# One inference step of a hybrid decoder layer: gate tiles in other buffers, a distance before one small sum, a fifth buffer for raw weights

## Chip, core and metric

The kernel runs on one core of one Trainium2 chip. The metric is the device time of one execution in microseconds (us). The engines are named as the profile names them: PE is TensorE, PEld its weight loads, DVE is VectorE, ACT is ScalarE, POOL is GpSimd and SP is SyncE, which here only issues DMAs.

## What is computed

One layer of a decoder for 512 prompt positions and 8 sampled positions that share all weights. Cut to what matters:

```python
xn = rmsnorm(h, norm_mix);  z = xn @ w_in
q, k, v of attention = parts of z (with rope);  o_a = dilated windowed attention, three groups mixed by softmax of lse
qm, km = silu(causal_conv(z parts));  vm, og = sigmoid(part of z);  i and f gates = 8 columns of z
C, n, m = stabilised mLSTM update;  hm = num / max(|den|, exp(-m));  o_b = rmsnorm(hm) * mh_norm * og
h += (sigmoid(z_ga) * (o_a @ w_proj_a) + sigmoid(z_gb) * (o_b @ w_proj_b)) @ w_out
x = rmsnorm(h, norm_ffn);  h += (silu(x @ w_gate) * (x @ w_up)) @ w_down
h += sigmoid(rmsnorm(h, norm_ple) @ w_ple_gate) * (p @ w_ple_proj);  y = rmsnorm(h, norm_final)
```

Beside y it returns the new key and value caches, the convolution rows and the mLSTM states of the prompt and of each sampled row.

## The kernel before

All activations lie transposed: 128 features on the partitions, 520 columns (512 prompt, 8 samples) along the free axis. Each float32 product is made of three PE products in the fp32r type: weight and activation are each split into a high part (a rounded copy, `whi`, `xnh`) and a low part (source minus high part, `wlo`, `xnl`), and high by high, high by low and low by high are summed in PSUM. So every chunk of weights (128x512) costs one cast on ACT or DVE and one subtraction on DVE before PE can use it, and every activation likewise.

The instruction order is not written by hand. A program, called the planner here, walks through a list of dense jobs (`order`, filled by `job`, `group` and `wino`) in `dense_to`. Beside that, generators (`Procs`) hold all the rest: evacuations, norms, attention, the mLSTM. Each generator yields a condition, and the planner goes on with it when the condition holds; it looks at them twice in every k step of a dense job (a k step is three products in two column halves, six matmuls). The conditions are made by `on(engines, *tiles, **rooms)`: there must be room in the named buffers, and all tiles must be ready by the time of the first named engine in the planner's own clock (`Clock`). For "pe" that time is the planner's PE time now. On the chip each engine then runs its own queue strictly in that order, and semaphores make it wait where the planner was too early. `used[tag]` counts the tiles of a buffer that are in use; `free(n, tag)` gives them back; a tag that is not in `used` is not counted.

The stages in order: the gate columns and four output gates on the unnormalised input (`n_pre`), with the squares of the eight input tiles for the first norm beside it (`first_norm`); `w_in` for attention and for the four mLSTM heads; eight `w_in` tiles of the mixing gates, whose Tanh goes to buffers by `RING` (`ev_tanh`); `w_proj_a` (`j_pa`, two chunks of two k steps in all) and `w_proj_b` in the form of seven products for two by two blocks (`wino`, `PRODS`), four groups q = 0 to 3, with eight more gate tiles after q = 0 and q = 1; `w_out`; `w_gate` and `w_up`; `w_down`; the last gate and the last norm.

Names that the steps touch:
- 24 small matmuls on `onesr` at the start keep PE busy until data is there.
- `first_norm`: for each input tile `xr[k]` one Square on ACT and one addition on DVE, then the norm `r0`, on which the first evacuations (`th<-pp,rb`) wait; two PSUM pairs (`pp`) are all that there is.
- `ev_tanh(tag, key)`: Tanh from PSUM into a tile of buffer `tag`, then the PSUM pair is free. For P1 and P2 it first waits until the sample states of head 3 have been loaded (`("loads", 3)`), since P1 and P2 hold the rows qb and kb for them.
- `on` and `op`: hold the attention outputs `o_sb` and `oaf`; later two tiles of `mix` each, and `hid` in the feed-forward part.
- `mk_oa` splits `oaf` into `oah` and `oal`.
- `sample_sums(h)`: for each head, the tile `nt` (five small DVE operations after the last `numv`), summed over partitions by four PE matmuls on `ones`; then `dns` on ACT and DVE and `sample_out`, which finishes the sampled columns of the gated output `th`. `mk_ob` then scales `th` and makes the operand `piece`s of `w_proj_b`.
- Raw weights of `w_proj_b` come in four blocks per group (11, 12, 21, 22) into buffers that are taken in turn (`wraws`): two of `rp`, one `cA`, one `cB`. A block is loaded when its buffer's last user has been split (`wlast`) and when it is at most seven chunks ahead. From the blocks DVE makes sums (`ws<-raw`, `raw<-raw,ws`), since four of seven products take sums of blocks.

Of the kernel before, what the change touches and what calls it, by code (L numbers as in the profile page):

```python
# [228 lines left out]
def _body(nc, a, const, sb, psp, drp):  # L229
# [5 lines left out]
              P1=2, P2=2, cm=2, on=2, W0=2, W1=2, W2=2, W3=2, hm=2, sm=4, sm48=4,  # L235
              pp=2, b1=4, hf=3)
    WIDTH = dict(cA=640, cB=512, W1=384, W2=256, W3=128, raw=512, hi=512, lo=512, zc=ZC, yc=ZC - 3)
    used = dict.fromkeys(("pp", "G", "WK", "b1", "z", "y", "zc", "yc", "S", "P1", "P2", "cm", "hm", "hf", "sw", "rp"), 0)

    def tl(tag, name, shape=None, dt=F32, count=True):  # L240
        w = WIDTH.get(tag, 520)
        if tag in used and count:
            used[tag] += 1
        return ck.new(sb.tile(list(shape or (128, w)), dt, name=name, tag=tag, bufs=NB[tag]), tag, NB[tag])
# [18 lines left out]
    def free(n, tag):  # L263
        used[tag] -= n
# [2 lines left out]

    P = dict(PAR["A"])

    def on(engs, *tiles, lim=None, **rooms):  # L270

        engs = engs.split()

        def ok():
            for tag, n in rooms.items():
                if tag in used and used[tag] + n > NB[tag]:
                    return False
            now = ck.t["pe"]
            for tag, n in rooms.items():
                i = ck.count.get(tag, 0)  # L280
                if any(ck.idle(tag, i + j, NB[tag]) > now + P["SLACK"] for j in range(n)):
                    return False
            if engs[0] == "pe":
                t = now
            else:
                t = min(ck.t[e] for e in engs)
                if t > now + (P["LIM"] if lim is None else lim):
                    return False
                t = max(t, now) + 0.1
            return all(ck.ready(x) <= t for x in tiles)  # L290
        return ok
# [265 lines left out]
        yield lambda: not left[0]  # L557

    split_at, dma_at, prep_at = [0], [0], [0]
    wraws, wlast = [Cycle(["rp"] * 2 + ["cA", "cB"])], {}  # L560
    raws, parts, kept, wok = {}, {}, {}, {}

    def dma_chunk():
# [205 lines left out]
    flag = {}  # L769
# [19 lines left out]
    ml = {}  # L789
# [242 lines left out]
    def ev_tanh(tag, key, scaled=True):  # L1032
        room = {tag: 1} if tag in used else {}

        def gen(ps):
            if tag in ("P1", "P2"):
                yield lambda: ("loads", 3) in flag
            if scaled:
                yield on("act", ps, lim=P["EVLIM"], **room)
                t = tl(tag, "th", (128, 520))  # L1040
                S_.activation(p2(t), ps, AF.Tanh, scale=0.5)
                free(1, "pp")
            else:
                yield lambda: "r0" in flag
                yield on("dve", rb, lim=P["EVLIM"], **room)
                t = tl(tag, "th", (128, 520))
                V.tensor_tensor(p2(t), ps, p2(rb), op=ALU.mult)
                free(1, "pp")
                yield on("act", t)
                S_.activation(t, t, AF.Tanh, scale=0.5)  # L1050
            ml[key] = t
        return gen
# [396 lines left out]
    def sample_sums(h, numv):  # L1449

        nn = nout[:, h, :, 1:9]
        w_i = s24b[:, h, 8:16].unsqueeze(1).to_broadcast([128, 2, 8])
        w_x = s24b[:, h, 0:8].unsqueeze(1).to_broadcast([128, 2, 8])
        nt = small(32, "nt").rearrange("p (t c) -> p t c", t=2)
        tv = nt[:, :, 0:8]
        V.tensor_tensor(tv, qkm[:, h, 1], w_i, op=ALU.mult)
        V.tensor_tensor(nn, nst[:, h], w_x, op=ALU.mult)
        V.tensor_tensor(nn, nn, tv, op=ALU.add)
        V.tensor_tensor(tv, nn, qkm[:, h, 0], op=ALU.mult)
        V.tensor_tensor(nt[:, :, 8:16], numv, numv, op=ALU.mult)  # L1460
        yield on("pe", nt, b1=1)
        bk = bank((128, 16))
        for t in range(2):
            PE.matmul(bk, ones, nt[:, t], start=t == 0, stop=t == 1)

        dn = sb.tile([128, 16], F32, name="dns", tag="dns", bufs=2)
        yield on("act", bk)
        S_.activation(dn[:, 0:8], bk[:, 0:8], AF.Abs)
        V.tensor_copy(dn[:, 8:16], bk[:, 8:16])
        free(1, "b1")  # L1470
        yield on("dve", dn)
        V.tensor_tensor(dn[:, 0:8], dn[:, 0:8], s24b[:, h, 16:24], op=ALU.max)
        ml["ns", h] = True
        yield lambda: ("og", h, 0) in ml and ("og", h, 1) in ml
        yield from sample_out(h, numv, dn)

    def mlstm_prompt(h):
# [36 lines left out]
        for s in range(4):  # L1514
# [18 lines left out]
            hi = tl(f"W{s}", f"W{s}h", None, F32R)[:, :n]  # L1533
# [13 lines left out]
        for vt in range(2):  # L1547
            c = slice(128 * vt, 128 * vt + 128)
            yield on("pe", W[0][1], b1=2 - vt)
            nu = bank()  # L1550
            if vt == 0:
                dn = bank()
            for s, (hi, lo, n) in enumerate(W):
                yield on("pe", lo)
                vh, vl = (x[:, s % 2, c] for x in ml["vt", h][s // 2])
                for j, (l_, r_) in enumerate(((vh, hi), (vh, lo), (vl, hi))):
                    PE.matmul(nu[:, TP - n:TP], l_, r_, start=(s == 0 and j == 0), stop=(s == 3 and j == 2))
            if vt == 0:
                for s, (hi, lo, n) in enumerate(W):
                    yield on("pe")  # L1560
                    for j, r_ in enumerate((hi, lo)):
                        PE.matmul(dn[:, TP - n:TP], onesr, r_, start=(s == 0 and j == 0), stop=(s == 3 and j == 1))
            yield on("act dve", nu, hm=1, y=1)
            hm = tl("hm", "hm")
            sq = tl("y", "sqh", (128, 512))
            copy(hm[:, :TP], nu)
            S_.activation(sq, nu, AF.Square)
            free(1, "b1")
            nums.append(hm)
            if vt == 0:  # L1570
                sqh = sq
                yield on("act", dn)
                free(1, "cm")
                da = tl("cm", "da")
                S_.activation(da[:, :TP], dn, AF.Abs)
                free(1, "b1")
                yield on("dve", da, emb)
                V.tensor_tensor(da[:, :TP], da[:, :TP], emb, op=ALU.max)
            else:
                yield on("dve", sq)  # L1580
                add(sqh, sqh, sq)
                free(1, "y")
# [5 lines left out]
        hi, lo = (tl("y", "sqh" + x, (128, 512), F32R) for x in "hl")  # L1588
        split(hi, lo, sqh)
        free(1, "y")  # L1590
        yield on("pe", hi, lo, b1=1)
        bk = bank()
        PE.matmul(bk, onesr, hi, start=True, stop=False)
        PE.matmul(bk, onesr, lo, start=False, stop=True)
# [52 lines left out]
    X0, X = (lambda: xs0), (lambda: xs)  # L1647
# [37 lines left out]
    j_mo(2, 1)  # L1685
    j_mo(3, 0)
    j_mo(3, 1)
    RING = ("zc", "yc", "P1", "P2")
    for m in range(4):
        for w in range(2):  # L1690
            j_w(50 + 8 * w + m, ev_tanh(RING[m % 4], ("g", w, m)))
# [15 lines left out]
    V.memset(ones, 1.0)  # L1707

    wb = bank((128, 128))
    for _ in range(24):  # L1710
        PE.matmul(wb, onesr, onesr, start=True, stop=True)
    free(1, "b1")
    warm = const.tile([128, 1], F32, name="warm")
# [24 lines left out]
    def first_norm():  # L1738
        for k in range(KD):
            yield on("act", xr[k], y=1)  # L1740
            sq = tl("y", "sq")
            square(sq, xr[k])
            if k == 0:
                acc = sq
                continue
            yield on("dve", sq)
            add(acc, acc, sq)
            free(1, "y")
        yield from norm(acc, "r0")
        yield from renorm(xr, gmix, "X", xs)  # L1750
        free(8, "G")
        yield lambda: order_pos[0] >= n_pre
        for t in X0T:
            free(1, t)
# [27 lines left out]
    def mk_oa():  # L1782
        yield lambda: 1 in oaf and "oas" in flag and "state3" in flag
        for i in range(2):
            yield on("act dve", oaf[i], WK=2)
            hi = tl("WK", "oah", None, F32R)
            lo = tl("WK", "oal", None, F32R)
            split(hi[:, :TP], lo[:, :TP], oaf[i])
            split(hi[:, TP:], lo[:, TP:], oas[:, i])
            oa.append((hi, lo))  # L1790

    mhh = const.tile([128, 8], F32, name="mhh")
    V.tensor_scalar(mhh, mh, 0.5, None, op0=ALU.mult)
# [12 lines left out]
            yield on("act dve", og[1], **(dict(G=7) if h < 3 else dict(S=5, hm=2)))  # L1806
            yield from pieces(*og, tags, obp)

    mixtags = ["on"] * 2 + ["op"] * 2 + ["W0"] * 2 + ["cm"] * 2 + ["X"] * 8

    def ev_pa(m):
        def gen(ps):
# [29 lines left out]
    def mix_parts(t, m):  # L1842
        if m > 3:
            yield lambda: order_pos[0] >= n_gates[0]
        yield on("act dve", t)
        mixp[m] = [tl(tag, "mix", (128, 520), F32R) for tag in mixtags[2 * m:2 * m + 2]]
        split(*mixp[m], t)
        free(1, "y")
# [5 lines left out]
        return {f"{r + 1}{k + 1}": a[name][2 * q + r, k] for r in range(2) for k in range(2)}  # L1854

    wok["rp"] = lambda: ("loads", 3) in flag and used["rp"] == 0
    wok["cA"] = lambda: "scores" in flag and "oas" in flag and ("ns", 3) in ml and 1 in oaf
    wok["WK"] = lambda: order_pos[0] >= n_pa

# [463 lines left out]
```

## Time and profile before

| | |
|---|---|
| median of 3 runs | 1076.74 us (1074.07 to 1078.79) |
| profiled execution | 1074.97 us |
| its span, first to last instruction | 1073.2 us |
| PE busy | 1043.7 us (97%) |
| PEld, DVE, ACT busy | 1019.7, 850.1, 517.7 us |
| bytes moved by DMA | 180.21 MB, mean 168 GB/s |
| granted clock, mean | 0.994 |

How to read it: the busy time of PE counts matmuls from issue to modelled end. Where PE's row of waits names an engine and a tile, PE had nothing to run until that tile was there. The granted clock is 1.00 at 2.4 GHz and 0.50 at 1.2 GHz. All lines are those of one helper (L224), so instructions are told apart by their tiles.

### The profile page before, as it was taken

To read this page: it belongs to the slowest core of one execution; us is meant where nothing else is said; L and a number is where in the kernel's file an instruction comes from. 1 tells how busy PE (TensorE), PEld (TensorE's weight loads), DVE (VectorE), ACT (ScalarE), POOL (GpSimd) and SP (SyncE) were. 2 spreads that over 40 slices of the span, in tenths; PEclk is the share of its full clock that TensorE was granted. 3 is DMA by queue.
4 is the path that set the end of the run, shared out by engine and by line. 5 is a ranking of instruction groups with operands and counts; after the bars stand their busy time and mean duration, and the time that the engine had idled before them with its cause. 6 is when DMAs were issued, how large, how long until landed. Compare 5 with 4: busy or idle time off the path is not lost.

```text
span 1073.2 us, 21731 instructions
## 1 busy us (share of the span) xinstructions
PE 1043.7 (97%) x8408; PEld 1019.7 (95%) x8408; DVE 850.1 (79%) x1756; ACT 517.7 (48%) x974; POOL 28.0 (3%) x110
## 2 busy tenths in 40 slices
PE   9999999999999989998999999999999999999996
PEld 9999999899987989998999999999999999999995
DVE  6994578958797799897467588989788888866685
ACT  6534554555565566665333245444344334433552
POOL 0010010000110100000000000000000000000000
PEclk9999999999999989999999999999999999999999
DMA  7366258765865967974766733422332332333331
GB/s 246 109 184 203 89 165 270 241 214 184 266 216 178 289 242 255 330 240 167 257 201 231 257 114 94 148 80 70 119 112 71 118 110 73 112 90 106 99 110 60
DMA packets 91191, 180.21 MB, mean 168 GB/s; under 512 B 11636, under 2 KB 37796, under 8 KB 89680
## 3 DMA queue, kind: packets, MB, share of 16 engines
q1 hardware_dynamic: 90512, 178.29, 51.4%
q8 instruction: 66, 1.08, 0.4%
q10 hardware_dynamic: 576, 0.53, 0.1%
q14 instruction: 37, 0.30, 0.1%
HBM read 163.65 MB, written 59.13 MB: 208 GB/s over the span
## 4 chain that ended last, share of the span: by engine, by line
PE 79%; DVE 11%; DMA 6%; ACT 2%; issue 2%; SPq 1%; DVEq 0%; ACTq 0%
PE pp L224 46%; PE b L224 33%; DVE wlo L224 2%; DMA raw<-in_w_in 2%; DMA out_C_s<-ct 2%; DMA ct<-in_sC 1%; DVE yc L224 1%; DVE ct L224 1%; DVE Wf L224 1%; DVE junk L224 1%; SPq L224 1%; DMA out_kvout<-in_cache 1%; DVE sw L224 1%; ACT whi L224 0%; DMA kb<-mdr 0%
## 5 line engine op out<-in xcount | busy, mean ns | idle before, releaser
L224 DVE TENSOR_TENSOR wlo<-raw,whi 128x512 fp32r<-128x512 f32 (+3 forms) x359 | 236.5, 661 | 138.2 <-ACT whi L224 125.1
L224 ACT CAST whi<-raw 128x512 fp32r<-128x512 f32 (+3 forms) x336 | 199.9, 598 | 298.2 <-PE pp L224 155.7
L224 PE MATMUL b<-piece,whi 128*128 128x260 f32 x1176 | 214.7, 284 | 3.9 <-ACT piece L224 2.0
L224 PE MATMUL pp<-xnh,whi 128*128 128x260 f32 x992 | 205.0, 288 | 0.0
L224 PE MATMUL pp<-xnh,wlo 128*128 128x260 f32 x992 | 203.0, 286 | 0.0
L224 PE MATMUL pp<-xnl,whi 128*128 128x260 f32 x992 | 200.3, 283 | 0.0
L224 PEld LDWEIGHTS b<-piece,whi 128*128 128x128 f32 x1176 | 182.8, 190 | 4.7 <-ACT piece L224 2.3
L224 PE MATMUL b<-piece,wlo 128*128 128x260 f32 x588 | 167.3, 284 | 0.1
L224 PEld LDWEIGHTS pp<-xnh,whi 128*128 128x128 f32 x992 | 153.5, 190 | 2.3 <-issue 0.9
L224 PEld LDWEIGHTS pp<-xnh,wlo 128*128 128x128 f32 x992 | 153.6, 190 | 2.1 <-issue 0.9
L224 PEld LDWEIGHTS pp<-xnl,whi 128*128 128x128 f32 x992 | 154.0, 190 | 0.0
L224 PEld LDWEIGHTS b<-piece,wlo 128*128 128x128 f32 x588 | 111.5, 190 | 0.4 <-DVE wlo L224 0.4
L224 PE MATMUL pp<-hph,wlo 128*128 128x260 f32 x352 | 70.9, 283 | 0.0
L224 PE MATMUL pp<-hpl,whi 128*128 128x260 f32 x352 | 70.8, 283 | 0.0
L224 PE MATMUL pp<-hph,whi 128*128 128x260 f32 x352 | 70.8, 282 | 0.0
L224 PEld LDWEIGHTS pp<-hph,whi 128*128 128x128 f32 x352 | 54.3, 189 | 0.0
L224 PEld LDWEIGHTS pp<-hpl,whi 128*128 128x128 f32 x352 | 54.3, 189 | 0.0
L224 PEld LDWEIGHTS pp<-hph,wlo 128*128 128x128 f32 x352 | 54.3, 189 | 0.0
L224 ACT CAST whi<-ws 128x512 fp32r<-128x512 f32 x28 | 17.4, 622 | 57.6 <-PE b L224 48.7
L224 DVE SCALAR_TENSOR_TENSOR yc<-zc,par,yc 128x552 f32<-128x552 f32 x48 | 37.7, 785 | 6.0 <-ACT yc L224 5.4
L224 DVE TENSOR_TENSOR uv<-uv,b 128x260 f32<-128x260 f32 (+1 forms) x84 | 40.8, 486 | 0.0
L224 PE MATMUL b<-x3h,wlo 128*128 128x260 f32 x128 | 36.7, 287 | 0.0
(393 smaller groups left out, 1918.9 us busy)
## 6 DMA issues: line engine op xcount, KB each, us to landing
raw<-in_w_in SPq DMA_DIRECT2D x132, 256.0 KB, 3.5
out_kvout<-in_cache SPq DMA_DIRECT2D x64, 512.0 KB, 6.3
raw<-in_w_gate SPq DMA_DIRECT2D x44, 256.0 KB, 2.7
raw<-in_w_up SPq DMA_DIRECT2D x44, 256.0 KB, 4.1
ct<-in_sC SPq DMA_DIRECT2D x32, 256.0 KB, 5.3
out_C_s<-ct SPq DMA_DIRECT2D x32, 256.0 KB, 5.1
raw<-in_w_down SPq DMA_DIRECT2D x32, 256.0 KB, 2.7
out_kvout<-in_cache SPq DMA_DIRECT2D x16, 510.0 KB
```

What stands on the lines that cost most here:

```text
L224: fn(*args, **kw)
```

## The change

Seven edits. (1) 18 small matmuls at the start in place of 24. (2) In `first_norm` the squares of tiles 6 and 7 are placed only after five chunks of weights have been split. (3) `on` gets an argument `lead`: for PE, the tiles must be ready `lead` us before the planner's PE time; it is 1.0 before the matmuls on `nt`, and 0.0 at two other places, which is as before. (4) `RING` is zc, yc, on, op in place of zc, yc, P1, P2, and the wait of `ev_tanh` for the loads of head 3 goes; `on` and `op` are now counted, and `mk_oa` gives back the three tiles of each that attention has taken. (5) The first four `mix` tiles lie in P1 and P2 and wait until the sums of head 3 are made. (6) The blocks of `w_proj_b` take five buffers in turn, with `sw` as the fifth. (7) `sw` may be taken for that once the states of head 3 are loaded and no tile of `sw` is in use.

```diff
-    used = dict.fromkeys((... "hf", "sw", "rp"), 0)
+    used = dict.fromkeys((... "hf", "sw", "on", "op", "rp"), 0)
...
-    def on(engs, *tiles, lim=None, **rooms):
+    def on(engs, *tiles, lim=None, lead=0.0, **rooms):
...
             if engs[0] == "pe":
-                t = now
+                t = now - lead
...
-    wraws, wlast = [Cycle(["rp"] * 2 + ["cA", "cB"])], {}
+    wraws, wlast = [Cycle(["rp"] * 2 + ["cA", "cB", "sw"])], {}
...
         def gen(ps):
-            if tag in ("P1", "P2"):
-                yield lambda: ("loads", 3) in flag
             if scaled:
...
-        yield on("pe", nt, b1=1)
+        yield on("pe", nt, lead=1.0, b1=1)
...
-    RING = ("zc", "yc", "P1", "P2")
+    RING = ("zc", "yc", "on", "op")
...
-    for _ in range(24):
+    for _ in range(18):
         PE.matmul(wb, onesr, onesr, start=True, stop=True)
...
             yield on("act", xr[k], y=1)
+            if k >= 6:
+                yield lambda: split_at[0] >= 5
             sq = tl("y", "sq")
...
             oa.append((hi, lo))
+        free(3, "on")
+        free(3, "op")
...
-    mixtags = ["on"] * 2 + ["op"] * 2 + ["W0"] * 2 + ["cm"] * 2 + ["X"] * 8
+    mixtags = ["P1"] * 2 + ["P2"] * 2 + ["W0"] * 2 + ["cm"] * 2 + ["X"] * 8
...
+        if m < 2:
+            yield lambda: ("ns", 3) in ml
         yield on("act dve", t)
         mixp[m] = [tl(tag, "mix", (128, 520), F32R) for tag in mixtags[2 * m:2 * m + 2]]
...
     wok["rp"] = lambda: ("loads", 3) in flag and used["rp"] == 0
+    wok["sw"] = lambda: ("loads", 3) in flag and used["sw"] == 0
```

## Rows read from the trace of the kernel before

**Rows 1.** The page: span, and the engines' busy time.
```profile
span 1073.2 us, 21731 instructions
PE 1043.7 (97%) x8408; PEld 1019.7 (95%) x8408; DVE 850.1 (79%) x1756; ACT 517.7 (48%) x974; POOL 28.0 (3%) x110
```

**Rows 2.** Waits of PE: who waited for whom, total us, times, longest.
```profile
PE b L224 <- DVE nt L224: 3.7, 1, 3.7
PE pp L224 <- DVE th L224: 2.3, 1, 2.3
PE b L224 <- ACT piece L224: 2.0, 1, 2.0
PE pp L224 <- ACT th L224: 2.0, 1, 2.0
PE b L224 <- DVE whi L224: 1.4, 1, 1.4
```

**Rows 3.** Four stretches: busy time by engine (count), granted clock, DMA share, GB/s.
```profile
25.00:32.00 7.00, 4.70 (x39) 4.52 (x39) 7.00 (x10) 4.83 (x7) 0.00 (x0) 1.00 0.25 75
376.00:387.00 11.00, 7.26 (x37) 7.06 (x36) 10.67 (x33) 6.60 (x15) 1.34 (x5) 0.69 0.73 261
387.00:390.00 3.00, 3.00 (x27) 3.00 (x26) 3.00 (x6) 1.76 (x4) 0.00 (x0) 1.00 0.41 123
500.00:510.00 10.00, 8.78 (x58) 8.58 (x59) 5.88 (x12) 3.73 (x6) 0.00 (x0) 0.83 0.27 85
```

**Rows 4.** Timeline of the start: start us, us, engine, operation, idle time before.
```profile
1.08 5.38 PE L224 MATMUL b<-onesr 128*128 128x128 f32 x24 [1.08 <-DVE onesr L224]
5.44 0.76 DVE L224 SCALAR_TENSOR_TENSOR x<-xr,par,x 128x520 fp32r<-128x520 f32 x1 [0.32 <-ACT x L224]
6.26 1.07 PE L224 MATMUL pp<-x,whi 128*36 128x260 f32 x4
9.51 0.75 DVE L224 SCALAR_TENSOR_TENSOR x<-xr,par,x 128x520 fp32r<-128x520 f32 x1
11.42 0.63 PE L224 MATMUL pp<-x,whi 128*128 128x260 f32 x4
```

**Rows 5.** Timeline of ACT: the fifth split, then the squares of the last tiles.
```profile
16.80 0.60 ACT L224 CAST whi<-raw 128x512 fp32r<-128x512 f32 x1
17.31 1.16 ACT L224 ACTIVATE sq<-xr 128x520 f32<-128x520 f32 x2
```

**Rows 6.** Chain that ended last, before nt of head 1: start us, us, what.
```profile
362.42 6.81 DMA ct<-in_sC
```

**Rows 7.** Timeline around nt of head 1.
```profile
380.12 0.17 DVE L224 TENSOR_TENSOR nt<-numv 128x16 f32<-128x16 f32 x1
380.34 1.04 PE L224 MATMUL b<-nt,onesr 128*128 128x16 f32 x4 [3.73 <-DVE nt L224]
```

**Rows 8.** Timeline of ACT: Tanh of the sixth mixing gate tile.
```profile
481.70 0.60 ACT L224 ACTIVATE th<-pp 128x520 f32<-128x520 f32 x1 [3.49 <-DVE numv L224]
```

**Rows 9.** Timeline: from nt of head 3 to the root of its dns.
```profile
483.14 0.52 PE L224 MATMUL b<-nt,onesr 128*128 128x16 f32 x4
486.23 0.16 DVE L224 SCALAR_TENSOR_TENSOR dns<-dns 128x8 f32<-128x8 f32 x1
487.13 1.28 ACT L224 ACT_TABLE_LOAD   x1
488.42 0.21 ACT L224 ACTIVATE dns<-dns 128x8 f32<-128x8 f32 x1
```

**Rows 10.** Timeline: loads, sums and splits of the last w_proj_b group.
```profile
577.82 1.05 SPq L224 DMA_DIRECT2D raw<-in_w_pb  x2
584.62 0.69 DVE L224 SCALAR_TENSOR_TENSOR th<-th,pp 128x520 f32<-128x520 f32 x1
586.44 0.68 DVE L224 TENSOR_TENSOR ws<-raw 128x512 f32<-128x512 f32 x1
587.89 0.43 DVE L224 CAST whi<-ws 128x512 fp32r<-128x512 f32 x1
```

More of the change, by code (lines that the diff above doesn't have):

```diff
@@ L237, in _body @@
     WIDTH = dict(cA=640, cB=512, W1=384, W2=256, W3=128, raw=512, hi=512, lo=512, zc=ZC, yc=ZC - 3)
-    used = dict.fromkeys(("pp", "G", "WK", "b1", "z", "y", "zc", "yc", "S", "P1", "P2", "cm", "hm", "hf", "sw", "rp"), 0)
+    used = dict.fromkeys(("pp", "G", "WK", "b1", "z", "y", "zc", "yc", "S", "P1", "P2", "cm", "hm", "hf", "sw", "on", "op", "rp"), 0)
     def tl(tag, name, shape=None, dt=F32, count=True):
@@ L1553, in mlstm_prompt @@
             for s, (hi, lo, n) in enumerate(W):
-                yield on("pe", lo)
+                yield on("pe", lo, lead=0.0)
                 vh, vl = (x[:, s % 2, c] for x in ml["vt", h][s // 2])
@@ L1590, in mlstm_prompt @@
         free(1, "y")
-        yield on("pe", hi, lo, b1=1)
+        yield on("pe", hi, lo, lead=0.0, b1=1)
         bk = bank()
```

## The prediction, made before the changed kernel was run

> **What bounds the kernel now.** Read the page first: PE is busy for 1043.7 of 1073.2 us [rows 1], and none of the seven edits takes a product out of it. So the change can only be worth what PE loses: 29.5 us in which it is not busy, and the stretches in which it runs at half clock. The waits of PE come next. The five longest are one event each and sum to 11.4 us [rows 2]; the rest is the start, the last norm and gaps of about 1 us or less. Then the granted clock by stretches. Over 376 to 387 us it is 0.69, which is 11 x 0.31 x 2 = 6.8 us at 1.2 GHz, right after the longest wait; over 500 to 510 us it is 0.83, some 3.4 us at 1.2 GHz, after the 2.0 us wait for `piece`; over 25 to 32 us it stays at 1.00, though the wait of 2.3 us lies inside [rows 2, 3]. At half clock half the time is lost, so the first drop costs about 3.4 us and the second 1.7 us. PE loses at `nt` of head 1 therefore 3.7 + 3.4 = 7.1 us, the largest single item, and it is the one that the change names.
>
> The profiled execution took 1074.97 us, 1.8 us over its span and 1.8 us under the median of 1076.74. I make the sum on 1074.97 and add 1.8 at the end.
>
> **The start (18 for 24 small matmuls, two squares later).** The 24 take 5.38 us, 0.224 each, so six fewer free PE at about 4.97 instead of 6.26 to 6.46 [rows 4]. The first activation's high part is there when DVE begins on its low part, 5.44, so at best PE starts 0.8 us earlier. It can't keep that: the low parts of the tiles follow one another on DVE and the fourth is there at 9.51 + 0.75 = 10.26, while PE still needs it and its own product for one k step. At the slow rate of the row at 6.26 (1.07 us for 4, some 0.22 from one start to the next) a k step of six takes 1.3 us, so PE would leave the fourth tile at about 11.3 to 11.4, where it is now, 11.42 [rows 4]. The later square is already placed so: the fifth split is at 16.80 and the last two squares follow at 17.31 [rows 5], so that the new condition keeps an order and makes none. I take -0.1 us. Bounds: -0.8 (the whole earlier start kept) and +1.7. The second is this: matmuls take 0.27 us each at 6.26 and 0.16 at 11.42, so the clock rises about there after PE has been at work from 1.08 without a break; with 18 there is a break of about half a us, and if the rise came later by a stretch as long as that of the second drop, 3.4 us at half rate, 1.7 us would go.
>
> The Trainium skill, TensorE: Matmul & The Clock Gate, section Why this matters for your kernels, speaks against this edit: it tells to keep TensorE busy without a break to get to the full clock. By it the term would be +1.7 and not -0.1. No row here shows a start with a break in it.
>
> **Tanh in on and op, mix in P1 and P2.** What goes is a wait on ACT: the Tanh of the sixth gate tile sits 3.49 us behind `numv` of head 3, because its P1 tile was still read by the sample steps [rows 8]. `on` and `op` are free long before, as `oaf` is split once the state of head 3 is done. Behind the waiting Tanh are casts of weights, for which PE doesn't wait at that place (no row of PE's waits names them there). The wait of PE that follows, 2.0 us for `th` [rows 2], ends with the last gate's Tanh behind two table loads on ACT, and these stay, since the root of head 3 stays between the two Tanhs. So 0, with bounds -2.0 (that wait goes) and +0.7 (the next cast or `wlo` moved in front of something PE needs, one operation of 0.7 us as the ones in [rows 10]). `mix` in P1 and P2 comes after the sums of head 3 in any case: 0.
>
> **The distance before nt.** `nt` of head 1 is ready at 380.29 and PE has waited 3.73 us for it [rows 7]. DVE is late because the state tile `ct` landed late: its load took 6.81 us [rows 6]. The edit doesn't speed that up. It moves the four matmuls behind at least 1.0 us more of PE's other work by the planner's clock; the planner looks twice in a k step, 6 x 0.11 = 0.67 us [rows 3], so 1.0 to 1.35, and I take 1.2. The wait shrinks to about 2.5 us. Bounds: nothing gained (DVE is later by as much), and everything, 3.7. The clock: a wait of 2.3 us left it at 1.00, one of 3.7 brought it to 0.50 [rows 2, 3], and 2.5 us is between them; the wait of 2.0 us at `piece` was enough there, in a stretch with another wait just after. I leave the drop in. The far bound is then -3.7 - 3.4 = -7.1.
>
> For the other heads PE was not late, so the edit only delays. Most is at stake in head 3: its sums run at 483.14, its `dns` is ready for the root at 486.4, and the root is taken at 488.42 after a cast and a table load that wait for nothing of it [rows 9]. That is 2.0 us of slack, and 1.2 us of delay fit into it: 0. If that cover is gone, each us late is one us more at the wait for `piece`, whose operands come from this chain, and a second half-clock stretch: +1.2 + 1.7 = +2.9 as the bound.
>
> **The fifth buffer.** It matters only where one group follows another closely, in the last one; the others have eight chunks of gate weights between. There PE waits 1.4 us for a `whi` cast from `ws` at 587.89, and `ws` was begun at 586.44, behind three operations of 0.6 us or so from the `th` at 584.62 on [rows 10]. The blocks 21 and 22 are issued at 577.82 now, each when its buffer's user is split. With five buffers they take `sw` and a tile of `rp` that were done with one product earlier, about 1.3 us (four k steps of three matmuls, 12 x 0.11 [rows 3]). The planner then can place the two sums ahead of two of these three operations: 1.2 us. The wait falls from 1.4 to about 0.4: -1.0. Bounds: -1.4, and +0.5 if the loads, which go past cache copies in SP's queue, land no earlier and only the order changes (half an operation of DVE). What is late next there is the operations that the sums pass, `th` and `mix`, which nobody needs before the next `w_out` job.
>
> **Sum.** -0.1 + 0 - 1.2 + 0 - 1.0 = -2.3 us: 1072.7 for a profiled execution, 1074.4 on the scale of the median. All bounds at once: -0.8 - 2.0 - 7.1 - 1.4 = -11.3 and +1.7 + 0.7 + 0 + 2.9 + 0.5 = +5.8.
>
> **Rivals.** *The clock stays up at nt.* If the shorter wait no longer drops the clock, 3.4 us more go: 1074.4 - 3.4 = 1071.0; with a wait cut to nothing by a new order, 2.5 more, 1068.5. For it: the 2.3 us wait at the start stage without a drop. Against it: the 2.0 us wait at `piece` with one. It decides at the length of the remaining wait, somewhere in 2.3 to 3.7 us. The same section of the skill's page asks for no long idle gaps between matmul bursts, since one sends the clock back; by that rule a shorter wait is on the safe side. The 3.7 us wait agrees with it, the 2.0 us one at `piece` doesn't.
>
> *Slower: head 3 comes late.* The delay of its `nt` passes the 2.0 us of slack, and the order on ACT turns so that the root and the last gate's Tanh each need another table load, 1.28 us each [rows 9]. Then the wait for `piece` grows by 1.2 + 2.6 us and the clock is down for a second stretch, 1.7: +5.5, 1079.9. It decides from 2.0 us of lateness on. For it: this chain already ends two of the five waits. Against it: ACT gets 3.49 us back in front of it [rows 8].
>
> *The edits do not do what they say.* The planner's times shift, DVE is as late at `nt` as before and the sums of the last group stay where they are: every gain is 0, the order of small things is shuffled by a us either way, 1076.7.
>
> **Chances.** The forecast 0.42 (its own range 1072 to 1077), the clock stays up 0.25 (1067 to 1072), no effect 0.18 (1075 to 1078.5), slower 0.15 (1078 to 1083). Under 1067 and above 1081 I leave together less than 2 in 10. A measurement of this kernel tells about 0.5% from no change, 5.4 us, that is from 1071.4 to 1082.1. Faster than that: most of the second case and a little of the first, 0.27. Slower than that: the upper end of the last case and new waits that a changed order makes, 0.11. Within: 0.62.
>
> **What would show it.** The wait for `nt` of head 1 at 2.3 to 2.7 us; a granted clock that still falls to half after it (right) or doesn't (the first rival); no wait on `numv` before a Tanh; the wait for `whi` from `ws` in the last group under 0.5 us; the first wait for `th` still 2 us or more with the norm's matmuls where they were; the wait for `piece` at about 2 us (more means the second rival). The prediction is wrong if the planner's order differs so much that the long waits stand at other tiles than these.

## The result and the profile after

The changed kernel takes 1066.27 us (median; 1065.44 to 1067.65), the kernel before 1077.24 us beside it (1074.07 to 1078.79): a ratio of 0.9914, with an interval of 0.9892 to 0.9935. By the ratio that is 9.3 us less (the two medians lie 11.0 apart), where 2.3 were forecast. The profiled execution took 1067.65 us and its span is 7.4 us shorter. All of this is PE's: its busy time is 2.3 us less (1043.7 in [rows 1]), 1.3 of it the six small matmuls that are gone, and its idle time 5.1 us less. The page of the kernel after begins so:

```profile
span 1065.8 us, 21726 instructions
PE 1041.4 (98%) x8402; PEld 1015.5 (95%) x8402; DVE 847.9 (80%) x1755; ACT 515.5 (48%) x973; POOL 33.5 (3%) x110
```

The waits of PE after (who waited for whom, total us, times, longest), to be read against [rows 2]:

```profile
PE b L224 <- DVE nt L224: 2.2, 1, 2.2
PE b L224 <- ACT qkm L224: 1.9, 2, 1.4
PE b L224 <- ACT sql L224: 1.2, 1, 1.2
PE b L224 <- DVE vml L224: 1.2, 1, 1.2
PE b L224 <- ACT sqhh L224: 1.1, 1, 1.1
```

Of the five long waits before, only `nt` is left, shorter. The wait for `th` at the start, `th` and `piece` near 490 to 500 us and `whi` in the last group are gone. New are `qkm` and `vml`, around 397 to 399 us, and `sql`, in the last norm.

The granted clock after (stretches, busy time by engine with count, clock, DMA share, GB/s), against [rows 3]:

```profile
192.00:196.00 4.00, 4.00 (x21) 3.94 (x22) 4.00 (x9) 2.25 (x3) 0.50 (x1) 0.57 0.64 190
376.00:387.00 11.00, 8.80 (x74) 8.60 (x74) 10.85 (x32) 7.33 (x15) 2.30 (x5) 1.00 0.60 212
387.00:405.00 18.00, 14.44 (x106) 12.89 (x104) 15.64 (x45) 11.99 (x27) 2.44 (x3) 1.00 0.75 235
500.00:510.00 10.00, 10.00 (x86) 10.00 (x85) 8.87 (x15) 3.40 (x6) 0.00 (x0) 1.00 0.43 138
```

The fall to 1.2 GHz at `nt` (0.69 before) and the one after `piece` (0.83) are gone; there is a new one at 192 to 196 us, 4 x 0.43 x 2 = 3.4 us at 1.2 GHz, after waits of 1.1 and 1.0 us for `sqhh` and `sqhl` of head 0, which the kernel before has too (1.0 and 1.0).

Where the time went is best read by setting the same instruction of PE in both traces side by side. Start in us:

| PE reaches | before | after | difference |
|---|---|---|---|
| first product of `w_in` on the norm's output | 40.60 | 38.21 | -2.4 |
| state product `W0h,vmh` of head 1 | 309.94 | 309.94 | 0.0 |
| first product of `j_pa` on `oah` | 489.58 | 488.51 | -1.1 |
| first `piece` of `w_proj_b` | 494.69 | 491.38 | -3.3 |
| `oah` of the second group | 532.23 | 524.98 | -7.3 |
| last product of `oah` and `whi` in the last group | 583.39 | 576.05 | -7.3 |
| first product of `w_out` on `mix` | 596.70 | 587.26 | -9.4 |
| first product of the last stage, on `x3h` | 1011.21 | 1002.71 | -8.5 |
| third of the last norm's four products on `sql` | 1064.02 | 1056.80 | -7.2 |

So the start's gain is lost again before head 1 (1.7 of it to the clock fall at 192 us). The step at `nt` leaves only 1.1 us at `j_pa`. **The largest part, 6.2 us, is gained between 488 and 525 us**, where `th`, `piece` and the clock fall after them stood. The last group adds 2.1. The last norm loses 1.0 at `sql` and 0.3 elsewhere; 0.9 us is lost in small steps between 620 and 1000 us, and I have no cause for that.

What stood behind the two waits can be seen on ACT. The rows of the kernel after, from the root of head 3 on (start us, us, engine, operation, idle before), answer to [rows 9]:

```profile
481.21 0.21 ACT L224 ACTIVATE dns<-dns 128x8 f32<-128x8 f32 x1 [1.07 <-DVE dns L224]
481.44 1.28 ACT L224 ACT_TABLE_LOAD   x1
482.73 0.21 ACT L224 ACTIVATE dns<-dns 128x8 f32<-128x8 f32 x1
482.96 1.28 ACT L224 ACT_TABLE_LOAD   x1
484.25 0.61 ACT L224 ACTIVATE th<-pp 128x520 f32<-128x520 f32 x1
488.99 0.60 ACT L224 ACTIVATE th<-pp 128x520 f32<-128x520 f32 x1
```

and the rows of PE at the first products of `j_pa`'s two chunks, after and then before:

```profile
488.51 0.40 PE L224 MATMUL pp<-oah,whi 128*128 128x260 f32 x2
489.93 0.41 PE L224 MATMUL pp<-oah,whi 128*128 128x260 f32 x2
```

```profile
489.58 0.40 PE L224 MATMUL pp<-oah,whi 128*128 128x260 f32 x2
493.14 0.51 PE L224 MATMUL pp<-oah,whi 128*128 128x260 f32 x2 [1.98 <-ACT th L224]
```

Before, the rows of ACT around the root (488.42 in [rows 9]) and from it on:

```profile
484.28 0.61 ACT L224 ACTIVATE th<-pp 128x520 f32<-128x520 f32 x1
489.31 1.35 ACT L224 ACTIVATE th<-th,mhh 128x520 f32<-128x520 f32 x2 [0.68 <-DVE th L224]
490.57 0.60 ACT L224 CAST whi<-raw 128x512 fp32r<-128x512 f32 x1
491.19 1.28 ACT L224 ACT_TABLE_LOAD   x1
492.49 0.60 ACT L224 ACTIVATE th<-pp 128x520 f32<-128x520 f32 x1
```

The root and the Tanh behind it still cost two table loads. What changed is which Tanh that is. Before, it was the last of the eight gate tiles: the seventh had run at 484.28, ahead of the root. The last Tanh empties the PSUM pair that the second chunk of `j_pa` needs; it began 2.9 us after the first product of `j_pa` (492.49 - 489.58), and PE waited 1.98 us. After, root and table loads stand **ahead of the seventh** Tanh (484.25). The last one has no table load in front of it and begins 0.5 us after the first product of `j_pa` (488.99 - 488.51), and PE doesn't wait. The whole of head 3 has moved forward on PE: its `W0h,vmh` from 453.00 to 442.31, its `nt` from 483.14 to 479.20. No edit asks for head 3 to come earlier. That shift is what the experiments had to explain.

### The profile page after: what moved, and what is told of

Read it like the earlier page. It is cut to its first block, busy times and chain, and to the rows that moved or that the text cites. A ratio compares the mean times of both kernels' runs of the same rounds, so it can differ in the third digit from the quotient of the medians.

```text
span 1065.8 us, 21726 instructions
## 1 busy us (share of the span) xinstructions
PE 1041.4 (98%) x8402; PEld 1015.5 (95%) x8402; DVE 847.9 (80%) x1755; ACT 515.5 (48%) x973; POOL 33.5 (3%) x110
## 4 chain that ended last, share of the span: by engine, by line
PE 56%; DVE 4%; DMA 2%; ACT 1%; issue 1%; SPq 0%; DVEq 0%; ACTq 0%
PE pp L224 30%; PE b L224 26%; DVE wlo L224 1%; DMA ct<-in_sC 1%; DMA out_kvout<-in_cache 1%; DMA raw<-in_w_in 1%; DVE ct L224 0%; DMA out_C_s<-ct 0%; SPq L224 0%; DVE h L224 0%; DVE junk L224 0%; DVE piece L224 0%; DVE da L224 0%; ACT whi L224 0%; DVE rb L224 0%
```

## The experiments

One theory: the distance in front of `nt` of head 1 changes the planner's order from there on, head 3 comes earlier, and the waits at 490 to 500 us fall for that reason. Its rival: the gain is what the edits name: the shorter wait at `nt` with its clock fall, the buffers of Tanh, the fifth buffer. Each kernel was timed in five rounds against the kernel before.

**The parts one at a time.** First the start alone:

```diff
-    for _ in range(24):
+    for _ in range(18):
...
+            if k >= 6:
+                yield lambda: split_at[0] >= 5
```

> The kernel before with 18 small matmuls in place of 24 and with the condition on the squares of tiles 6 and 7; nothing else. The prediction's working says -0.1 us and that the wait of 2.3 us for th at 29 us stays. The other theory, from the changed kernel's trace (matmuls of the first norm at 20.1 us in place of 22.6, no wait for th, PE 2.4 us ahead from 29 us on): the shorter start turns the order so that the squares come earlier, PE is 2.4 us ahead by 60 us; at the end -2.4 us, or some -0.8 us if the waits around sqhh of head 0 near 190 us bring the clock down for 3.4 us as they do there.

Measured: 1075.63 us, 0.9987 (0.9970 to 1.0004). The wait for `th` at 29 us is gone, and PE stands 2.0 us ahead at 40 us. The waits at `nt` (4.0), `piece` (2.0) and `th` (2.0) and the fall at `nt` stay. The interval of the time still holds 1. What moved PE forward in the trace is on DVE: the two reciprocals of the first norm, 3.4 us, begin at 22.0 in place of 23.8, since squares and additions were turned ahead of splits; before, DVE had nothing to do for 2.2 us there and was busy without a break in 25 to 32 us [rows 3]. The rows, with the start alone and then before:

```profile
22.01 3.41 DVE L224 RECIPROCAL rb<-rb 128x260 f32<-128x260 f32 x2
```

```profile
23.76 3.41 DVE L224 RECIPROCAL rb<-rb 128x260 f32<-128x260 f32 x2 [2.23 <-ACT rb L224]
```

The distance alone, for all heads:

```diff
-    def on(engs, *tiles, lim=None, **rooms):
+    def on(engs, *tiles, lim=None, lead=0.0, **rooms):
...
-                t = now
+                t = now - lead
...
-        yield on("pe", nt, b1=1)
+        yield on("pe", nt, lead=1.0, b1=1)
```

> The kernel before with lead=1.0 in front of the matmuls on nt; nothing else. The prediction's working: the wait for nt of head 1 falls from 3.7 to 2.5 us, the clock still falls to half behind it, the waits for th (2.0) and piece (2.0) near 493 and 501 us stay: -1.2 us. The other theory, that the distance turns the order after head 1 and brings head 3 forward: wait for nt near 2.2 us without a drop of the clock (-1.5 and -3.3), new waits of some 3.6 us between 393 and 404 us, nt of head 3 about 4 us earlier, and the waits for th and piece with the drop behind them gone (-6): together -7 us or so, a ratio near 0.993.

Measured: 1069.48 us, 0.9933 (0.9906 to 0.9959): 7.2 us, most of the change. Yet the fall of the clock at `nt` is there in full. Its waits of PE and the clock at `nt`:

```profile
PE pp L224 <- DVE th L224: 2.3, 1, 2.3
PE b L224 <- DVE nt L224: 2.3, 1, 2.3
PE b L224 <- DVE whi L224: 1.4, 1, 1.4
```

```profile
376.00:387.00 11.00, 8.70 (x48) 8.49 (x48) 10.85 (x31) 7.38 (x15) 2.30 (x5) 0.69 0.56 202
```

The rows for `piece` and for `th` behind ACT are missing, though the buffers of Tanh are as before. So neither the clock at `nt` nor the buffers are needed for this gain. At 487 us PE does the same `w_in` products at the same time as before, within 0.1 us, but `nt` of head 3 stands 3.0 us earlier among them, and at 509 us PE is 5.9 us ahead.

The buffers of Tanh alone (with the count of `on` and `op`, `free`, and the wait of `mix` as in the change):

```diff
-            if tag in ("P1", "P2"):
-                yield lambda: ("loads", 3) in flag
...
-    RING = ("zc", "yc", "P1", "P2")
+    RING = ("zc", "yc", "on", "op")
```

> The kernel before with the Tanh tiles of the mixing gates in on and op, the first mix tiles in P1 and P2 and the counting that goes with it; nothing else, and the order of instructions on each engine is that of the kernel before. The prediction: ACT no longer waits 3.5 us for numv at 478 to 482 us, and the time doesn't change (0, bounds -2.0 and +0.7). The other theory, that ACT's late Tanh is what holds up the chain of head 3: the waits for th and piece near 493 and 501 us and the drop of the clock behind them shrink or go, up to -6 us.

Measured: 1077.68 us, 0.9999 (0.9982 to 1.0016). The row of [rows 8] has lost its wait: that Tanh runs at 480.99 without one for `numv`. PE's waits are what they were:

```profile
PE b L224 <- ACT piece L224: 2.0, 1, 2.0
PE pp L224 <- ACT th L224: 2.0, 1, 2.0
```

The fifth buffer alone:

```diff
-    wraws, wlast = [Cycle(["rp"] * 2 + ["cA", "cB"])], {}
+    wraws, wlast = [Cycle(["rp"] * 2 + ["cA", "cB", "sw"])], {}
...
+    wok["sw"] = lambda: ("loads", 3) in flag and used["sw"] == 0
```

> The kernel before with the fifth buffer for raw rows of w_proj_b; nothing else. The prediction: the wait of 1.4 us for whi from ws near 588 us falls to about 0.4 us, -1.0 us. By the changed kernel's trace, where PE gains 2.1 us between the last w_proj_b group and the first w_out matmul: -1.4 to -2.1 us and no wait for whi there. If the group's sums stay where they are: 0.

Measured: 1074.42 us, 0.9975 (0.9957 to 0.9993), 2.7 us. No wait for `whi` is left in the last group. In the kernel after, DVE shows why:

```profile
575.13 0.69 DVE L224 TENSOR_TENSOR ws<-raw 128x512 f32<-128x512 f32 x1
575.85 0.69 DVE L224 TENSOR_TENSOR ws<-ws,raw 128x512 f32<-128x512 f32 x1
576.46 0.68 DVE L224 TENSOR_TENSOR wlo<-raw,whi 128x512 fp32r<-128x512 f32 x1
577.06 0.69 DVE L224 SCALAR_TENSOR_TENSOR th<-th,pp 128x520 f32<-128x520 f32 x1
```

Both sums now stand ahead of both `th`, where they stood behind `th`, `mix` and `th` [rows 10].

The four ratios give 1.4 + 7.2 + 0.1 + 2.7 = 11.4 us against 9.3 for the whole; within the intervals, which are 2 to 3 us to either side, the parts add up.

**Which head's distance it is.** The edit of the distance with `lead` only at head 1:

```diff
-        yield on("pe", nt, b1=1)
+        yield on("pe", nt, lead=(1.0 if h == 1 else 0.0), b1=1)
```

> The kernel before with the distance of 1.0 for nt of head 1 alone. In the instruction order nt of head 1 then stands 10 matmuls later and the state matmuls of head 3 stand 78 dense matmuls earlier (some 9 us), as with the distance for all heads. If the gain of the distance is this turn of the order: about the same -7 us (ratio 0.993), no waits of 2 us for th and piece near 490 to 500 us. If it needs the distance at head 3 or the others too: less than half of it.

Measured: 1068.50 us, 0.9913 (0.9894 to 0.9931). And only at the others:

```diff
-        yield on("pe", nt, b1=1)
+        yield on("pe", nt, lead=(0.0 if h == 1 else 1.0), b1=1)
```

> The kernel before with the distance of 1.0 for nt of heads 0, 2 and 3 and not of head 1. In the instruction order these three stand 6 dense matmuls later and nothing else on PE moves. The prediction's step: 0.7 us of delay at head 3 fit into its slack, so no change (0). The prediction's rival: head 3 late, the wait for piece grows by 0.7 us or more: +0.7 to +2.4. If the gain of the distance is at these heads: -7.

Measured: 1076.57 us, 0.9988 (0.9971 to 1.0005). All of the distance's gain comes from head 1. At head 3 the distance turns two steps on ACT: the last Tanh (494.77) now runs ahead of the scaling of `th` (495.27), which stood 3.2 us ahead of it before. PE pays 2.7 in place of 2.0 us at `piece` and 1.0 in place of 2.0 at `th`: nothing in sum.

**Is it head 3's place?** Now the changed kernel, with the prompt part of head 3 held back in the list of dense jobs:

```diff
+        if h == 3:
+            yield lambda: order_pos[0] >= 101
```

> The changed kernel with the prompt part of head 3 held back to a given chunk, so that its state and score matmuls stand where they stood in the kernel before (some 78 dense matmuls later than in the changed kernel), while nt of head 3 comes 64 dense matmuls earlier. If the early prompt part of head 3 is what removed the waits for th and piece: they come back in part or whole, +2 to +6 us over the changed kernel (1068 to 1072). If only the early nt (the sampled rows) matters: no such waits, within 1 us of the changed kernel.

Measured: 1068.49 us, 0.9912 (0.9895 to 0.9929). The state products of head 3 are late (`W0h,vmh` at 453.48, as before), but its `nt` is early, 474.13, and no wait for `th` or `piece` comes back. So the early state isn't needed. One job later:

```diff
+        if h == 3:
+            yield lambda: order_pos[0] >= 102
```

> The same with head 3 held back one chunk more: score matmuls of head 3 102 dense matmuls later than in the changed kernel, and nt of head 3 30 later, 6 later than in the kernel before. If head 3's place is the cause, by either part: waits of 2 us or more for th or piece in front of or within the first w_proj_b group, +4 to +8 us over the changed kernel (1070 to 1074). If the place of head 3 is not the cause: within 1 us of the changed kernel.

Measured: 1077.06 us, 0.9997 (0.9985 to 1.0010): the whole gain is gone, with `nt` of head 3 at 484.26. Waits of PE for `th` (1.0) and `piece` are back, and the clock with them:

```profile
PE b L224 <- ACT piece L224: 2.7, 1, 2.7
```

```profile
500.00:510.00 10.00, 8.91 (x48) 8.62 (x49) 4.92 (x10) 3.11 (x5) 0.00 (x0) 0.66 0.10 31
```

That is 10 x 0.34 x 2 = 6.8 us at 1.2 GHz, 3.4 us of loss, and 7.1 us with the two waits. This kernel also had half-clock stretches at 381 and 398 us, 3.4 us long each, which lose 3.4 us together, so not every us of the difference belongs to head 3.

Then `nt` of head 3 alone, from the kernel with the distance at head 1 only (0.9913):

```diff
-        yield on("pe", nt, b1=1)
+        yield on("pe", nt, lead=(0.0, 1.0, 0.0, 6.0)[h], b1=1)
```

> The kernel with the distance of 1.0 at head 1 alone, and in it nt of head 3 alone put off (distance 6.0): it stands 48 dense matmuls later, some 5.8 us, 6 behind its place in the kernel before; nothing else on PE moves, the prompt part of head 3 stays early. If the place of head 3's sums is what removes the waits for th and piece: they come back, 3 to 4 us of waits and on most executions a drop of the clock behind them, ratio about 0.996 to 0.998 in place of 0.991. If the early prompt part is what counts: 0.991 stays.

Measured: 1070.05 us, 0.9939 (0.9914 to 0.9963). `nt` of head 3 runs at 483.22, where it ran before the change, and one wait is back:

```profile
492.08 0.51 PE L224 MATMUL pp<-oah,whi 128*128 128x260 f32 x2 [1.56 <-ACT th L224]
```

on a Tanh of ACT that again stands behind a late root:

```profile
490.12 1.28 ACT L224 ACT_TABLE_LOAD   x1
491.42 0.60 ACT L224 ACTIVATE th<-pp 128x520 f32<-128x520 f32 x1
```

The wait for `piece` is not back. Its source, the scaled `th` (`th<-th,mhh`), was done by 488.75, against 490.67 before, and ACT casts it into `piece` ahead of the last Tanh. Before, the casts stood behind that Tanh. The rows, with `nt` of head 3 late and before:

```profile
488.66 0.92 ACT L224 CAST piece<-th 128x260 fp32r<-128x260 f32 x2
```

```profile
492.99 0.93 ACT L224 CAST piece<-th 128x260 fp32r<-128x260 f32 x2
```

This order tells all fourteen kernels apart: PE waits 2.0 to 2.7 us for `piece` in the seven with these casts behind the last Tanh, and not in the seven with the casts ahead of it (in two of these on DVE). An early `th` is not enough: with 4.0 at head 1 (below) it was scaled 0.2 us ahead of `j_pa`, as here, the casts still stood behind the last Tanh, and PE waited 2.7 us. By the traces the late `nt` alone costs 1.6 us of waiting, and both waits with the clock some 7. By the times it costs 2.8 us (0.9913 to 0.9939, intervals that overlap).

One difference tells in all fourteen kernels how long PE waits for `th`. It is the start of the last gate's Tanh on ACT, less the start of `j_pa`'s first product on PE:

| kernel | last Tanh - `j_pa`, us | wait for `th`, us |
|---|---|---|
| before; start alone; buffers alone; fifth buffer alone | +2.9 each | 2.0 each |
| `nt` of head 3 late; 18 small matmuls alone (below) | +2.5; +2.5 | 1.6; 1.6 |
| distance at heads 0, 2, 3; head 3 from 102; 4.0 at head 1 (below) | +1.9 each | 1.0 each |
| distance at head 1 only; changed kernel with it at head 1 only (below) | +1.0; +1.0 | under 0.1 |
| after; distance alone; head 3 from 101 | +0.5; +0.6; +0.5 | none |

The wait is this difference less 0.9 us, to within 0.1 us, wherever there is one. In the first three rows both table loads of the root stand between the seventh and the last Tanh, in the last two rows both stand ahead of the seventh.

**Is it the length of the distance?** Four us at head 1 take the wait for `nt` away altogether:

```diff
-        yield on("pe", nt, b1=1)
+        yield on("pe", nt, lead=(4.0 if h == 1 else 0.0), b1=1)
```

> The kernel before with a distance of 4.0 for nt of head 1 alone: it stands 28 dense matmuls later (some 3.4 us), and by the order nt of head 3 is 12 matmuls later than in the kernel before, so that head 3 gains nothing. The wait at nt of head 1 should fall under 0.8 us and the clock should stay up behind it. By the prediction's own mechanism that alone is worth 3 to 3.7 us and 3.4 us of clock: ratio 0.994 to 0.997. By the theory that the gain is head 3's: the waits for th and piece stay, and the sum is near 0.996; if the wait at nt is worth nothing at all: 1.000.

Measured: 1078.43 us, 1.0018 (0.9999 to 1.0036). PE has no wait at `nt`, and gains nothing. Rows of PE:

```profile
382.31 0.51 PE L224 MATMUL b<-nt,onesr 128*128 128x16 f32 x4
387.89 0.54 PE L224 MATMUL pp<-xnh,whi 128*128 128x260 f32 x2 [1.87 <-ACT whi L224]
389.59 0.80 PE L224 MATMUL pp<-xnh,wlo 128*128 128x260 f32 x2 [0.72 <-DVE wlo L224]
```

```profile
387.00:396.00 9.00, 7.38 (x37) 7.08 (x38) 8.62 (x22) 5.90 (x16) 2.81 (x3) 0.62 1.00 351
```

PE ran on into the next weights, which weren't split yet, and waited there; the clock fell as well (0.62 over 9 us, 6.8 us at 1.2 GHz). Head 3 came late (`nt` at 488.86), and the waits for `th` and `piece` are back. PE also waits 2.6 us at 487 us for the Tanh of [rows 8], on which ACT stood 2.87 us behind `numv`. This trace is of the longest of the twelve executions (1082.31 us, mean clock 0.988; the shortest took 1073.57 at 0.995), so it has more clock falls than others. What it shows all the same: the wait at `nt` is not in itself worth its length. Without the new order of head 3 its time was lost at the next tiles that were late, `whi` and `wlo`, 2.6 us in sum.

**The start without the condition.** With 18 small matmuls and nothing else:

```diff
-    for _ in range(24):
+    for _ in range(18):
```

> The kernel before with 18 small matmuls in place of 24 and without the condition on the squares. The order changes on PE from the start on. If the condition only keeps an order that is there anyway (the prediction's step): within 1 us of the kernel with both (ratio 0.9987). If it is needed: the squares of tiles 6 and 7 come before splits that PE needs, a wait of 1 us or more in the first 30 us, and with the order changed over many stages a time that can lie 3 us to either side.

Measured: 1082.56 us, 1.0054 (1.0034 to 1.0074), slower. Without the condition the squares go ahead of the splits, PE waits 0.5 and 1.1 us for `whi` and `wlo` at 18 to 20 us, and what it won by the `th` of the first norm is gone. The planner's order then differs as far as head 3, with one very long wait:

```profile
485.78 0.80 PE L224 MATMUL pp<-xnh,whi 128*128 128x260 f32 x2 [10.28 <-ACT th L224]
```

```profile
485.12 0.60 ACT L224 ACTIVATE th<-pp 128x520 f32<-128x520 f32 x1 [3.17 <-DVE numv L224]
```

This is the wait of [rows 8], a Tanh into P1 or P2 behind `numv` of head 3. Here PE's other work doesn't cover it.

**The changed kernel with the distance at head 1 only.**

```diff
-        yield on("pe", nt, lead=1.0, b1=1)
+        yield on("pe", nt, lead=(1.0 if h == 1 else 0.0), b1=1)
```

> The changed kernel with the distance at head 1 alone in place of all heads. Head 3's sums stand 18 dense matmuls earlier than in the changed kernel. If the gains add: 0.991 of the distance at head 1, 0.9975 of the fifth buffer and 0.9987 of the start give 0.9877, some 1063.5 us, 2 to 4 us under the changed kernel. If the changed kernel already has all there is at head 3: the same as the changed kernel, 0.990 to 0.992.

Measured: 1064.94 us (1064.07 to 1065.86), 0.9890 (0.9869 to 0.9911), the best of all, though its interval overlaps that of the change (0.9892 to 0.9935). Its clock stays up at 192 us and its last norm has no wait of 1.2 us for `sql`, but 3.4 us at 1.2 GHz come back after `nt`, where it waits 2.8 us. Twice, then, the distance at head 1 only came out ahead of that at all heads: 0.9913 against 0.9933 in the kernel before, 0.9890 against 0.9914 in the changed one, 2.2 and 2.6 us. The intervals overlap in both pairs, so a price of the distance at the other heads is possible and not shown.

## Why the prediction was right or wrong

It forecast 1074.4 us, -2.3 us, and a difference too small to be told from none as the likeliest case. The sign was right, the size a quarter of what was measured, the ratio 0.9914 is beyond 0.5%, and 1066.27 lies just under 1067, the lower end of its fastest case. That the sign came out is in part luck: the largest part of the gain came by a path that the sum didn't have. By its steps:

- **What bounds the kernel: right in the main.** The gain came from PE's waits and its clock. But an edit does take products out: six small matmuls, 1.3 us of PE's busy time (5.4 us for 24, 4.1 for 18). Calling `nt` "the largest single item" was right as a reading of the rows, and misleading as a place to look for the gain: the two waits of 2.0 us near 490 to 500 us with their clock fall (2.0 + 2.0 + 1.7, [rows 2, 3]) hang together and fell together.
- **The start, -0.1: the step that failed is "the new condition keeps an order and makes none".** That holds with 24 small matmuls: there the planner makes the same instructions in the same order with the condition as without it. With 18 it turns the squares ahead of the splits; the two edits are one. Together they bring -2.0 us at 40 us, outside the bounds, because the `th` of the first norm is no longer late, and -1.4 in the whole time, with an interval of -3.2 to +0.4 that can't tell it from -0.1; 18 without the condition cost 5.8 us. The bound of +1.7 from a late rise of the clock didn't come: PE's break ahead of 5.34 us is 0.15 us and not half a us, and the clock rose at 11.2 us after, 11.4 before. Over all traces it rose at 9.8 to 12.7 us in the six kernels with 18 and at 8.1 to 11.4 in the eight with 24, 1.2 us later in the mean, which at half rate would be some 0.6 us; the scatter is wider than that. (18 matmuls by its own 0.224 us end at 5.11, not 4.97; nothing hangs on it.) The "first wait for `th` still 2 us or more" was the test, and it failed.
- **Tanh's buffers, 0: right**, with the reason given, for this edit by itself: the wait on `numv` went and PE's waits stayed. That "the root of head 3 stays between the two Tanhs" failed in the change all the same, since head 3 came forward; the two table loads stayed, but ahead of both. What the wait on `numv` costs where its cover is gone was seen twice (10.28 us of PE with 18 small matmuls alone, 2.56 us with 4.0 at head 1; ACT stood 3.17 and 2.87 us on `numv`). The bounds of -2.0 and +0.7 didn't reach for that.
- **The distance, -1.2: the mechanism at `nt` was right, and it was the smaller part; the step that failed is the order behind it.** The matmuls moved behind ten more of PE's products, 10 x 0.12 = 1.2 us, as worked out, and the wait fell from 3.7 to 2.2 (2.1 to 3.4 in the other kernels that have it at 1.0). DVE was as late as said (`nt` at 380.34 after, 380.12 before). What failed is that for the other heads "the edit only delays". Delaying `nt` of head 1 altered all that the planner placed after it: head 3 came forward by 4 to 11 us, and 7.2 us went (all from head 1). The sum took the order as fixed and moved single instructions in it, though the kernel's order is computed: a term for "the order after this point is another" was missing, and the only row that could have bounded it was the 5.7 us of waits and clock at 490 to 510.
- **The clock at `nt`: left in by the forecast, and the first rival had it go.** In the kernel after it went (1.00 after a wait of 2.2 us); with the distance at head 1 only it stayed (3.4 us at 1.2 GHz after 2.6), with the same ratio (0.9913 and 0.9914), and with the distance at all heads too (0.69 after 2.3). "It decides at the length of the remaining wait" is wrong: 2.2 us was followed by no fall, 2.07 us by one. The Trainium skill, TensorE: Matmul & The Clock Gate, section Why this matters for your kernels, asks for no long idle gaps between matmul bursts; waits in that sense short, 2.07 us in the kernel with `nt` of head 3 late, were followed by half clock (0.84 over 376 to 387), so the trace doesn't bear it out as a safe side.
- **Head 3, 0, and the rival "slower": the time was right, the slack was not, and the rival had the right place.** The distance at heads 0, 2 and 3 alone costs nothing that can be measured. But the 2.0 us of slack didn't hold: the scaling of `th` came behind the last Tanh, and the wait for `piece` grew by 0.7 us, while that for `th` fell by 1.0. A head 3 that comes late costs what the rival named, the two waits and a longer clock fall: 7.1 us in the kernel with head 3 from 102, of the 9 us between it and the change. The change moved head 3 the other way.
- **The fifth buffer, -1.0: mechanism right, undersized.** The sums passed three operations, not two, the wait went from 1.4 to nothing that counts, and `w_out` begins 2.1 us sooner; 2.7 us (0.8 to 4.6 by the interval) by the time.

## What to carry to other kernels

Where a program computes the instruction order, an edit in one place can move instructions far behind it: before costing one by moving single instructions in the old trace, build the new order and see which instructions stand elsewhere, and what each long wait late in the trace hangs on. Two waits that follow one chain (here the last Tanh and the casts into `piece`, both behind one root) are worth their sum and the clock behind them, and the number to watch is the distance between the producer on one engine (the last Tanh on ACT) and the consumer on the other (`j_pa` on PE). When reading it, make sure that both traces show the same instance of the producer: here the Tanh behind the root was the eighth before and the seventh after. A wait moved away from one place is not gained if the engine that was late is still late at the next tile, as the 4.0 us at head 1 showed.

## What the runs showed of the hardware

The length of PE's wait doesn't tell whether the clock falls, nor for how long. After waits at `nt` of 2.20, 2.30, 2.58, 2.93, 3.42 and 4.0 us the stretch at 1.2 GHz was 0, 6.8, 3.4, 6.8, 3.4 and 6.8 us. The same wait of 2.3 us at the start left the clock at 1.00 in the kernel before [rows 3], and brought it to 0.76 over 25 to 32 us in the kernel with the distance at heads 0, 2 and 3. Two waits of 1.1 and 1.0 us, 0.5 us apart, were followed by a fall at 192 us in the kernel after, but two of 1.0 and 1.0 us were not in the one with the distance at head 1. What decides it these runs don't show. Of every such stretch half was lost, 1.7 or 3.4 us, so of two executions with the same waits one can be that much longer. The kernel with the buffers alone has the order of the kernel before on PE and the same long waits there, yet its trace has two more falls of 3.4 us (at 458 and 496 us), and it took 4.3 us more. Among 29 executions of the kernel before, the shortest (1073.29 us) had a mean clock of 0.993 and the longest (1081.09 us) one of 0.988. A gain of a few us is therefore read from the median of several executions, and one trace tells where waits went, not how much the clock gave.
